# Feed-forward blocks of an encoder trunk: one plain chunk in place of two, and two seven-product chunks opened by p1 and p2

## The chip, the cores and the metric

The kernel runs on one core of a Trainium2 chip. TensorE multiplies matrices, VectorE and ScalarE work element by element, GpSimd (POOL in the profile) and SyncE (SP) mostly issue DMAs here. The metric is the device time of one execution in microseconds (us), the median of several runs. All arithmetic that matters is in float32.

## The reference, cut to what matters

Two batches of tokens, 512 and 256 long, run through two layers with shared weights. Each layer is a feed-forward block, a token mixer, and a second feed-forward block:

```python
def swiglu_ffn(x, w1, w2):
    gate, up = jnp.split(x @ w1, 2, axis=-1)
    return (jax.nn.silu(gate) * up) @ w2
...
x = x + 0.5 * swiglu_ffn(rmsnorm(x, norm_g[li, 0]), ffn_w1[li, 0], ffn_w2[li, 0])
...
x = x + 0.5 * swiglu_ffn(rmsnorm(x, norm_g[li, 2]), ffn_w1[li, 1], ffn_w2[li, 1])
```

The model width is 1024 and the hidden width 2816. So there are four feed-forward blocks, called f0, f1, f2 and f3 here and in the code; the mixers stand between f0 and f1 and between f2 and f3.

## The kernel before, in words

All 768 tokens are worked on at once, split into two halves of 384. A float32 product is made of three fast ones: each operand is split into a high part, rounded to the fast type by a ScalarE copy, and a low part, which VectorE gets by subtracting the high part from the original. TensorE then accumulates high x high, high x low and low x high (`mm3`, and the inner loop of `product`, L522). Line numbers are those of the profile.

**Chunks.** The first multiplication of a feed-forward block goes by 22 chunks of 128 hidden columns. A chunk has a gate part and an up part. There are two kinds:

- A *plain* chunk (`up_plain`, L499) multiplies gate and up for one token half at a time: 2 products over 8 slices of the width, 3 matmuls each, for each of two halves. Its weights are two pieces of 128x1024, each split at once (`plain_steps`, L176).
- A *seven-product* chunk (`up_pair`, L536) takes gate and up by the two halves of the width, and these by the two token halves, as a 2x2 block product, and does it in seven products, p1 to p7, in place of eight, Strassen-Winograd fashion. Each product runs over 4 slices of the width. Each needs one token operand (`FACTOR`, L47): the plain blocks b00, b10, b11, or the mixed ones t1 to t4; and one weight operand, one of the four blocks a11, a12, a21, a22 or a sum of them.

**Weights of a seven-product chunk** (`quad_steps`, L199). Two loads (`wr` tiles, four buffers) bring gate and up. A third load brings a21 a second time (`s3`, two buffers), and two accumulating DMAs on GpSimd's queue (L153) add a11 into `s3` for p7 and a22 into a21. Two VectorE additions (L243) make the operands of p6 (a11 += a21) and p3 (a12 += a11) in place. Each of the seven operands is split: ScalarE cast at L229, VectorE subtraction at L230, into one `w` tile. There are eight `w` tiles. `ahead` stages the next operand whenever a `w` tile is counted free, so the program's order of staging follows the `done` calls of the products.

**Token operands.** At the start of a block the normalized tokens are transposed on TensorE, scaled, and split (`turn`, L398 on; the splits are `put`, whose copy and subtraction are L293 and L294). One call does one half of the width for one half of the tokens. Then `sums` (L450) makes the mixed operands: `mix` (L439) does four subtractions per half of the inner slices (L441, L442, L444, L445) and splits t1, t4, t3 and t2 in this order (L294), all on tiles of 128x768. In f0 two more additions of 128x768 (L453) stand ahead of it. `turn` and `sums` are queued in `self.deferred`, and `run_later` takes one at a time, at set places between the matmuls.

**The order at the start of a block** (`ffn`, L673 on). Chunks 0 and 1 (`PLAIN = 2`) are plain: chunk 0 half 0, chunk 1 half 0, chunk 0 half 1, chunk 1 half 1. While the first 96 matmuls run, the second token half is turned and `sums` is handed in; the b01 and b11 operands are first needed by the second 96. Then come chunks 2 and 3 as seven-product chunks in the order `UP` (p1, p7, p2, p5, p4, p6, p3). The four chunks' results are mixed in the same way (`gather`) for the second multiplication (`down_quad`, L581 on, matmuls at L608), which itself is in seven products per group of four chunks. The remaining 18 chunks are seven-product chunks in four more groups of four and a last pair.

**Who decides the order on an engine.** The program is written in one sequence, and the order of the instructions on each engine is fixed when it is built: of those that can go, the one written first goes first, and one written later gets in where the earlier ones would have to wait. `tc.issue_after(i)` holds an instruction behind `i` on `i`'s engine.

Of the kernel before, what the change touches and what calls it, by code (L numbers as in the profile page):

```python
# [12 lines left out]
AF = mybir.ActivationFunctionType  # L13
# [3 lines left out]
P = 128  # L17
D = 1024
DFF = 2816
NC = D // P  # L20
NF = DFF // P
# [14 lines left out]
H = T // 2  # L36
HB = H // P
PLAIN = 2
GROUPS = (NF - PLAIN) // 4
WBUFS = 8  # L40
# [3 lines left out]
WARM = 21  # L44
UP = ("p1", "p7", "p2", "p5", "p4", "p6", "p3")
DOWN = ("p1", "p2", "p5", "p4", "p7", "p6", "p3")
FACTOR = {"p1": "b00", "p2": "b10", "p3": "b11", "p4": "t4", "p5": "t1", "p6": "t2", "p7": "t3"}  # L47


class Trunk:  # L50
# [104 lines left out]
    def load_next(self):  # L155
# [43 lines left out]
    def quad_steps(self, key, raws, srcs, order):  # L199
# [35 lines left out]
        own = {"p1": [a11], "p2": [a12], "p3": [a12], "p4": [a22], "p5": [a21], "p6": [a11], "p7": s3}  # L235
        sums = {"p6": (a11, a21), "p3": (a12, a11)}
        last = [None]

        def step(name):
            if name in sums:  # L240
                into, term = sums[name]
# [156 lines left out]
    def turn(self, half, part, row):  # L398
# [61 lines left out]
    normed = mixed = first = halved = None  # L460
    normal = None
    plains = 0
# [73 lines left out]
    def up_pair(self, tag, j, hold=False):  # L536
        nc = self.nc
        key = (tag, j)
        a, b, c, d = (self.ps(H) for _ in range(4))
# [8 lines left out]
        self.tail = None  # L548
        p("p7", c, True, False)
        nc.scalar.copy(w, c)  # L550
        free("p7")
        p("p2", a, False, True)
        nc.scalar.activation(a, a, AF.Silu)
        free("p2")
        p("p5", d, True, False)
        nc.vector.tensor_sub(w, w, d)
        free("p5")
        p("p4", c, False, True)
# [4 lines left out]
        free("p4", "p6")  # L563
        yield t
# [13 lines left out]
        free("p3")  # L578
        yield w

    def down_quad(self, tag, g, hid):  # L581
# [91 lines left out]
    def ffn(self, tag, next_row):  # L673
        for g in range(GROUPS):
# [7 lines left out]
            def gather(ts, kp):  # L682
                self.mix(ts[0], ts[1], ts[2], ts[3], lambda name, src: put(name, src, kp))

            if g == 0:
                ts = {}
                for half in range(2):
                    for j in range(PLAIN):
                        t = ts[2 * j + half] = self.up_plain(tag, j, half)
                        name = f"b{j}{half}"  # L690
                        if name != "b01":
                            low = put(name, t, 0)
                        if name == "b00" and self.whole:
                            with self.tc.issue_after(low):
                                for parts in self.whole[:2]:
                                    self.nc.vector.tensor_add(*parts)
                            del self.whole[:2]
                gather(ts, 0)
                self.run_later(len(self.deferred))
            for kp in range(2):  # L700
                if g == 0 and kp == 0:
                    continue
                ts = []
                for j in range(2):
                    for half, t in enumerate(self.up_pair(tag, 4 * g + 2 * kp + j, j == 0)):
                        ts.append(t)
                        name = f"b{j}{half}"
                        if name != "b01":
                            put(name, t, kp)
                gather(ts, kp)  # L710
# [868 lines left out]
```

## Time and profile before

| | |
|---|---|
| median of 3 runs | 2731.82 us (2731.79 to 2732.84) |
| span of the profiled execution | 2730.5 us |
| TensorE busy | 2720.2 us, 17305 matmuls |
| VectorE busy | 2110.3 us |
| ScalarE busy | 1339.0 us |
| GpSimd busy | 204.8 us |

The span is the time from the first to the last instruction in one profiled execution; the runs are timed from outside. In the profile's rows an instruction stands with its line, engine, operation, the tiles that it writes and reads, its shape and a count; behind the bar are busy time and the mean duration of one. In a timeline, a row begins with its start in us from the span's start and the time that it covers; a bracket at the end tells how long the engine had been idle before it and what ended that. ACT is ScalarE, DVE VectorE, PE TensorE's matmuls and PEld its weight loads. Tiles: `big` are token operands, `wr` and `s` raw weights, `w` split weights, `ps` PSUM banks, `tA` intermediate results.

### The profile page before, as it was taken

The page shows a single profiled execution, that of the slowest core. Times are in us where ns is not written, and L with a number is a line of the kernel's source. Part 1 is how long each engine was busy: PE and PEld are TensorE (multiplying, and loading weights), DVE is VectorE, ACT ScalarE, POOL GpSimd, SP SyncE. Part 2 cuts the span into 40 slices and gives each one's busy share as a digit, 9 for nine tenths or more (in the row PEclk, how much of TensorE's full clock was granted, in tenths as well). Part 3 has the DMA queues.
Part 4 walks back from the last instruction along what each step waited for, and adds up shares of the span by engine and source line. Part 5 has one row for each costly group of instructions (what it writes and reads, how often), then busy time and mean ns, then how long its engine had stood idle before and what let it go on. Part 6 is the DMA issues. An engine that isn't in the chain of part 4 may idle for free.

```text
span 2730.5 us, 44549 instructions
## 1 busy us (share of the span) xinstructions
PE 2720.2 (100%) x17305; PEld 2483.8 (91%) x17305; DVE 2110.3 (77%) x3789; ACT 1339.0 (49%) x2507; POOL 204.8 (7%) x243
## 2 busy tenths in 40 slices
PE   9999999999999999999999999999999999999998
PEld 9999999889888889999999999999987789999998
DVE  8888788567476778778888878887847768787877
ACT  6444444456466554444446444444546754444443
POOL 1110110000000000111110011101000000111000
PEclk9999999999999999999999999999999999999999
DMA  6544554311110524465553355544422123555443
GB/s 183 136 123 117 127 143 120 123 56 48 55 41 25 143 65 120 113 147 129 128 121 102 88 129 139 135 116 112 133 72 78 47 62 87 130 139 135 117 112 108
DMA packets 331411, 293.98 MB, mean 108 GB/s; under 512 B 11752, under 2 KB 258240, under 8 KB 331200
## 3 DMA queue, kind: packets, MB, share of 16 engines
q1 hardware_dynamic: 294352, 212.89, 26.6%
q0 software_dynamic: 32544, 64.76, 13.6%
q10 hardware_dynamic: 4304, 13.49, 1.4%
q8 instruction: 135, 2.21, 0.3%
q14 instruction: 76, 0.62, 0.1%
HBM read 216.91 MB, written 9.44 MB: 83 GB/s over the span
## 4 chain that ended last, share of the span: by engine, by line
PE 97%; DVE 1%; ACT 1%; issue 0%; DMA 0%; DVEq 0%; SPq 0%; ACTq 0%
PE ps L527 42%; PE ps L608 21%; PE ps L288 9%; PE ps L289 9%; PE ps L290 9%; PE ps L856 1%; PE ps L643 1%; PE ps L1451 1%; PE ps L1442 1%; PE ps L1004 1%; PE ps L1390 1%; PE ps L411 1%; PE ps L980 0%; PE ps L969 0%; DVE x L671 0%
## 5 line engine op out<-in xcount | busy, mean ns | idle before, releaser
L527 PE MATMUL ps<-big,w 128*128 128x384 f32 x6720 | 1169.7, 334 | 0.6 <-ACT tA L544 0.6
L527 PEld LDWEIGHTS ps<-big,w 128*128 128x128 f32 x6720 | 1165.9, 188 | 2.8 <-ACT tA L544 1.2
L229 ACT CAST w<-wr 128x512 fp32r<-128x512 f32 (+1 forms) x606 | 424.2, 710 | 721.8 <-DVE wr L243 305.4
L230 DVE TENSOR_TENSOR w<-wr,w 128x512 fp32r<-128x512 f32 (+1 forms) x606 | 480.5, 798 | 225.4 <-ACT w L229 158.5
L608 PE MATMUL ps<-w,big 128*128 128x512 f32 x2520 | 575.4, 389 | 0.0
L608 PEld LDWEIGHTS ps<-w,big 128*128 128x128 f32 x2520 | 472.8, 188 | 97.5 <-DVE x L671 0.3
L671 DVE SCALAR_TENSOR_TENSOR x<-ps,x 128x512 f32<-128x512 f32 x468 | 302.6, 681 | 4.7 <-PE ps L290 4.7
L288 PE MATMUL ps<-w,big 128*128 128x512 f32 x576 | 232.5, 404 | 0.0
L290 PE MATMUL ps<-w,big 128*128 128x512 f32 x576 | 225.5, 391 | 0.0
L289 PE MATMUL ps<-w,big 128*128 128x512 f32 x576 | 225.1, 391 | 0.0
L288 PE MATMUL ps<-big,w 128*128 128x384 f32 (+2 forms) x640 | 217.9, 342 | 0.2
L289 PE MATMUL ps<-big,w 128*128 128x384 f32 (+2 forms) x640 | 215.8, 337 | 0.4 <-DVE big L371 0.2
L290 PE MATMUL ps<-big,w 128*128 128x384 f32 (+2 forms) x640 | 215.1, 336 | 0.0
L293 ACT CAST big<-tA 128x384 fp32r<-128x384 f32 x296 | 147.8, 512 | 117.5 <-DVE tA L572 40.4
L153 POOL DMA_DIRECT2D s<-wr x122 | 106.3, 913 | 1300.1 <-DMA wr<-in_ffn_w_dram 623.6
L189 DVE TENSOR_TENSOR w<-wr,w 128x1024 fp32r<-128x1024 f32 (+1 forms) x88 | 105.9, 1209 | 82.0 <-ACT w L186 73.4
L294 DVE TENSOR_TENSOR big<-tA,big 128x384 fp32r<-128x384 f32 x296 | 159.9, 551 | 8.2 <-ACT big L293 7.8
L153 POOL DMA_DIRECT2D wr<-wr x101 | 87.6, 868 | 1009.3 <-DVE tA L1110 386.0
L186 ACT CAST w<-wr 128x1024 fp32r<-128x1024 f32 (+1 forms) x90 | 93.0, 1035 | 93.4 <-PE ps L289 66.3
L288 PEld LDWEIGHTS ps<-w,big 128*128 128x128 f32 x576 | 108.3, 188 | 25.6 <-issue 4.6
L290 PEld LDWEIGHTS ps<-w,big 128*128 128x128 f32 x576 | 108.1, 188 | 23.5 <-issue 0.4
L289 PEld LDWEIGHTS ps<-big,w 128*128 128x128 f32 x640 | 121.0, 189 | 9.4 <-DVE big L294 1.0
(191 smaller groups left out, 2891.8 us busy)
## 6 DMA issues: line engine op xcount, KB each, us to landing
wr<-in_ffn_w_dram SPq DMA_DIRECT2D x264, 512.0 KB, 3.9
s<-wr POOLq DMA_DIRECT2D x122, 256.0 KB, 5.1
s<-in_ffn_w_dram SPq DMA_DIRECT2D x120, 256.0 KB, 3.3
wr<-wr POOLq DMA_DIRECT2D x80, 256.0 KB, 4.2
wr<-in_hg_w_in_dram SPq DMA_DIRECT2D x40, 512.0 KB, 3.8
wr<-wr POOLq DMA_DIRECT2D x21, 512.0 KB, 6.0
spill<-x ACTq DMA_DIRECT2D x12, 512.0 KB, 2.9
x<-spill ACTq DMA_DIRECT2D x12, 512.0 KB, 3.3
```

The source lines that it names most:

```text
L153: self.nc.gpsimd.dma_start(out, src, accum_op=ALU.add)
L189: eng.tensor_sub(lo, raw[:, ks, :], hi.bitcast(F32))
L229: nc.scalar.copy(h, src)
L230: low = nc.vector.tensor_sub(l, src, h.bitcast(F32)).ins
L288: nc.tensor.matmul(out, a[0], b[0], start=first, stop=False)
L289: nc.tensor.matmul(out, a[0], b[1], start=False, stop=False)
L290: nc.tensor.matmul(out, a[1], b[0], start=False, stop=last)
L293: self.nc.scalar.copy(hi, src)
L294: return self.nc.vector.tensor_sub(lo, src, hi.bitcast(F32)).ins
L527: self.nc.tensor.matmul(ps, a[x], b[y], start=first and k == 0 and i == 0, stop=k == 3 and i == 2, skip_group_check=True,)
L608: nc.tensor.matmul(ps, a[x], w[y], start=name == chain and kp == 0 and q == 0, stop=kp == 1 and q == 2, skip_group_check=True,)
L671: return self.nc.vector.scalar_tensor_tensor(x, ps, c, x, ALU.mult, ALU.add).ins
```

## The change

Chunk 1 becomes a seven-product chunk too. Chunks 1 and 2 are opened together by the new function `open_pair`: p1 and p2 of both need only b00 and b10, so they take the place of the plain chunk 1's half 0. Behind plain chunk 0's half 1 come the rest, crossed: p3 of chunk 1, p3 of chunk 2, p5, p7 of chunk 1, p5 of chunk 2, p4, p6 of chunk 1, p7 of chunk 2, then p6 and p4 of chunk 2. Since p3 now runs before p6, both weight additions are made ahead of p3, held behind the last subtraction of `turn` (`self.turned`). The staging of these operands is barred (`self.closed`) until the first product of chunk 0's half 1 is done. Chunk 3 takes its products in the order `THIRD`, with p4 second and p7 fourth. The places at which `run_later` is called move with the products that stand there: of the six calls in the first 96 matmuls, four are now behind p1 and p2 of the two chunks. The bank and the intermediate tiles of the pair are used in another order, with p3 opening the bank that p5 closes.

```diff
-PLAIN = 2
-GROUPS = (NF - PLAIN) // 4
+GROUPS = (NF - 2) // 4
...
+OPEN = ("p1", "p2", "p3", "p5", "p7", "p4", "p6")
+OPEN2 = ("p1", "p2", "p3", "p5", "p7", "p6", "p4")
+THIRD = ("p1", "p4", "p2", "p7", "p5", "p6", "p3")
...
-        self.loaded.append((len(raws), steps))
+        if how is OPEN:
+            self.loaded.append((2, steps[:2]))
+            self.opened = steps[2:]
+        elif how is OPEN2:
+            a, b = self.opened, steps[2:]
+            self.loaded.append((0, steps[:2]))
+            self.closed = (2, [a[0], b[0], a[1], a[2], b[1], a[3], a[4]])
+            self.loaded += [self.closed, (2, b[2:])]
+        else:
+            self.loaded.append((len(raws), steps))
...
-        sums = {"p6": (a11, a21), "p3": (a12, a11)}
+        sums = {"p6": [(a11, a21)], "p3": [(a12, a11)]}
+        if order in (OPEN, OPEN2):
+            sums = {"p3": sums["p6"] + sums["p3"]}
...
-                with self.tc.issue_after(last[0]):
+                low = self.turned if order in (OPEN, OPEN2) else last[0]
+                with self.tc.issue_after(last[0]), self.tc.issue_after(low):
                     nc.vector.tensor_add(into, into, term)
...
+            if self.loaded[0] is self.closed:
+                return
...
             low = self.put(name, kp, self.tn[(part, half)][:, kp])
+            self.turned = low
...
-            if i < PLAIN:
+            if i == 0:
...
-                self.plan_quad((tag, i), (gate, up), (NC, P), UP)
+                self.plan_quad((tag, i), (gate, up), (NC, P), {1: OPEN, 2: OPEN2, 3: THIRD}.get(i, UP))
...
-                if half == 0 and k in (((), (2, 6)), ((3, 7), (3, 7)))[j][c]:
+                if half == 0 and c and k in (2, 6):
                     self.run_later()
             if half:
+                self.closed = None
                 self.done((tag, j, c))
...
+    def open_pair(self, tag, j, hold):
...
+        def gate():
+            p("p1", "a", True, False)
+            nc.scalar.copy(v, banks["a"])
+            free("p1")
+            self.run_later()
+            p("p2", "a", False, True)
+            nc.scalar.activation(banks["a"], banks["a"], AF.Silu)
+            free("p2")
+            self.run_later()
+
+        def p3():
+            p("p3", "d", True, False)
+            nc.scalar.copy(w, banks["d"])
+            free("p3")
+
+        def p5():
+            p("p5", "d", False, True)
+            free("p5")
...
             if g == 0:
...
+                gate, p3, p5, p7, p4, p6, results = zip(*(self.open_pair(tag, j, j == 2) for j in (1, 2)))
+                gate[0]()
+                gate[1]()
+                first.append(self.up_plain(tag, 0, 1))
                 self.run_later(len(self.deferred))
+                for step in (p3[0], p3[1], p5[0], p7[0], p5[1], p4[0], p6[0], p7[1]):
+                    step()
+
+                def second():
+                    p6[1]()
+                    p4[1]()
+                    yield from results[1]()
```

Left out of the diff above are `open_pair`'s p7, p4, p6 and its results, which combine the banks by the same sums and differences as `up_pair` does, and the two places of `up_pair` where chunk 3's p4 and p7 are exchanged.

More of the change, by code (lines that the diff above doesn't have):

```diff
@@ L537, in up_pair @@
         nc = self.nc
+        third = j == 3
         key = (tag, j)
@@ L548, in up_pair @@
         self.tail = None
-        p("p7", c, True, False)
+        p("p4" if third else "p7", c, True, False)
         nc.scalar.copy(w, c)
-        free("p7")
+        free("p4" if third else "p7")
         p("p2", a, False, True)
@@ L554, in up_pair @@
         free("p2")
+        if third:
+            p("p7", c, False, True)
+            nc.vector.tensor_sub(w, c, w)
+            free("p7")
         p("p5", d, True, False)
@@ L557, in up_pair @@
         free("p5")
-        p("p4", c, False, True)
+        if not third:
+            p("p4", c, False, True)
         p("p6", b, True, True)
@@ L562, in up_pair @@
         nc.vector.tensor_mul(t, t, a)
-        free("p4", "p6")
+        free(*(("p6",) if third else ("p4", "p6")))
         yield t
@@ L579, in up_pair, with p, free, p7 @@
         yield w
+    def open_pair(self, tag, j, hold):
+        nc = self.nc
+        banks = {}
+        v, w = (self.tmp(H) for _ in range(2))
+        def p(name, bank, first, last):
+            if first:
+                banks[bank] = self.ps(H)
+            self.product((tag, j), name, FACTOR[name], banks[bank], first, last)
+        def free(name):
+            self.done((tag, j, name))
+        def gate():
[14 more added lines that the diff above has]
+            free("p5")
+        def p7():
+            p("p7", "c", True, False)
+            nc.vector.tensor_add(w, w, banks["c"])
+            nc.vector.tensor_sub(w, w, banks["d"])
+            free("p7")
+        def p4():
+            p("p4", "c", False, True)
+            free("p4")
+        def p6():
+            p("p6", "b", True, True)
+            nc.vector.tensor_sub(v, v, banks["b"])
+            free("p6")
+        def results():
+            t = self.tmp(H)
+            nc.vector.tensor_sub(t, banks["c"], v)
+            nc.vector.tensor_mul(t, t, banks["a"])
+            yield t
+            nc.vector.tensor_sub(w, w, v)
+            nc.vector.tensor_add(v, v, banks["d"])
+            def finish(after=None):
+                with self.tc.issue_after(after) if after else nullcontext():
+                    self.last_act = nc.scalar.activation(v, v, AF.Silu).ins
+                self.last_dve = nc.vector.tensor_mul(w, v, w).ins
+            if hold:
+                self.tail = finish
+            else:
+                finish()
+            yield w
+        return gate, p3, p5, p7, p4, p6, results
     def down_quad(self, tag, g, hid):
@@ L683, in gather @@
                 self.mix(ts[0], ts[1], ts[2], ts[3], lambda name, src: put(name, src, kp))
+            pairs = {}
             if g == 0:
[L686 to L697, printed above, removed]
@@ L698, in ffn @@
-                gather(ts, 0)
-                self.run_later(len(self.deferred))
+                first = [self.up_plain(tag, 0, 0)]
+                low = put("b00", first[0], 0)
+                if self.whole:
+                    with self.tc.issue_after(low):
+                        for parts in self.whole[:2]:
+                            self.nc.vector.tensor_add(*parts)
+                    del self.whole[:2]
+                gate, p3, p5, p7, p4, p6, results = zip(*(self.open_pair(tag, j, j == 2) for j in (1, 2)))
```

14 lines of the change are left out of this document (7 added, 7 removed).

## The prediction

> **What bounds the kernel now.** I read the page first, then the shapes kept apart, then the timelines around the starts of the four feed-forward blocks.
>
> ```profile
> span 2730.5 us, 44549 instructions
> PE 2720.2 (100%) x17305; PEld 2483.8 (91%) x17305; DVE 2110.3 (77%) x3789; ACT 1339.0 (49%) x2507; POOL 204.8 (7%) x243
> L527 PE MATMUL ps<-big,w 128*128 128x384 f32 x6720 | 1169.7, 334 | 0.6 <-ACT tA L544 0.6
> PE ps L104 <- DVE eps L101: 1.1, 1, 1.1
> ```
>
> TensorE is busy for all but 10 us of the span, before the commonest matmul it idled 0.6 us in 6720, and its longest wait, the first row of the waits, is 1.1 us at the very start. So an instruction taken from TensorE is worth its whole pace, until TensorE has to wait. The mean of 334 ns is no pace, since neighbours overlap: 1169.7 us / 6720 = 0.174 us from one to the next. The plain chunks' matmuls have the same shape.
>
> ```profile
> 48.35 29.28 PE L527 MATMUL ps<-big,w 128*128 128x384 f32 x168
> 77.47 28.90 PE L608 MATMUL ps<-w,big 128*128 128x512 f32 x126
> 1030.91 29.28 PE L527 MATMUL ps<-big,w 128*128 128x384 f32 x168
> 1520.87 19.40 PE L527 MATMUL ps<-big,w 128*128 128x384 f32 x111
> 2272.07 18.19 PE L527 MATMUL ps<-big,w 128*128 128x384 f32 x104
> ```
>
> These rows of TensorE's timeline show where, in blocks f0 to f3, the plain chunks end and chunk 2 begins. The first gives the pace again: (77.47 - 48.35) / 168 = 0.173 us. The question is what VectorE does just before, since it makes everything that TensorE reads here.
>
> **The saving.** A plain chunk takes 2 halves x 2 products x 8 x 3 = 96 matmuls, a seven-product chunk 7 x 4 x 3 = 84. Chunk 1 changes kind in four blocks: 4 x 12 x 0.1735 us = 8.3 us. This is certain, and it is the ceiling.
>
> **What moves earlier.** In the old order TensorE runs 192 plain matmuls and then p1 of chunk 2 before it needs a mixed operand (t3, for p7). In the new one it runs 96 matmuls (plain half 0, then p1 and p2 of chunks 1 and 2), 48 of plain half 1, and then p3 of chunk 1, p3 of chunk 2, p5 with t1, p7 with t3. So the plain part ends 48 x 0.1735 = 8.3 us earlier than the five rows say: at 40.0, 1022.6, 1512.5 and 2263.7 us. There p3 of chunk 1 starts. Its third matmul reads the low weight half, so that must exist at 40.4. P3 of chunk 2 starts 12 x 0.1735 = 2.1 us later and needs its low half at 42.4, 1025.0, 1515.0 and 2266.2.
>
> **What p3 costs VectorE.** Two additions (L243), a ScalarE cast, then a subtraction (L230). The change lets the additions start only behind the last operand written by `turn`, and both chunks' p3 are staged in the program behind `sums`, because `closed` opens only after the first plain product of half 1. So, who goes first on VectorE when both are ready?
>
> ```profile
> 35.94 0.62 ACT L229 CAST w<-wr 128x512 fp32r<-128x512 f32 x1 [4.63 <-issue]
> 30.42 1.82 DVE L294 TENSOR_TENSOR big<-big,big 128x768 fp32r<-128x768 f32 x2
> 32.16 1.82 DVE L453 TENSOR_TENSOR big<-big 128x768 f32<-128x768 f32 x2
> 33.90 1.81 DVE L441 TENSOR_TENSOR big<-big,big 128x768 f32<-128x768 f32 x2
> 35.64 1.82 DVE L442 TENSOR_TENSOR big<-big,big 128x768 f32<-128x768 f32 x2
> 37.38 0.95 DVE L444 TENSOR_TENSOR big<-big,big 128x768 f32<-128x768 f32 x1
> 38.24 0.95 DVE L294 TENSOR_TENSOR big<-big,big 128x768 fp32r<-128x768 f32 x1
> 39.11 0.94 DVE L445 TENSOR_TENSOR big<-big,big 128x768 f32<-128x768 f32 x1
> 39.98 0.94 DVE L444 TENSOR_TENSOR big<-big,big 128x768 f32<-128x768 f32 x1
> 40.85 0.54 DVE L519 TENSOR_TENSOR tA<-tA,ps 128x384 f32<-128x384 f32 x1
> 41.97 3.57 DVE L294 TENSOR_TENSOR big<-big,big 128x768 fp32r<-128x768 f32 x4 [0.57 <-ACT big L293]
> 45.45 0.95 DVE L445 TENSOR_TENSOR big<-big,big 128x768 f32<-128x768 f32 x1
> 46.32 0.68 DVE L230 TENSOR_TENSOR w<-wr,w 128x512 fp32r<-128x512 f32 x1
> 46.92 0.68 DVE L230 TENSOR_TENSOR w<-s,w 128x512 fp32r<-128x512 f32 x1
> 47.52 2.69 DVE L294 TENSOR_TENSOR big<-big,big 128x768 fp32r<-128x768 f32 x3
> 50.13 0.55 DVE L294 TENSOR_TENSOR big<-tA,big 128x384 fp32r<-128x384 f32 x1
> ```
>
> This is block f0. The pair at 30.42 ends `turn`; from 32.16 to 50.13 VectorE works off `sums`. The first weight of chunk 2, which the old program stages at the place where the new one stages p3, was cast at 35.94, and its subtraction came at 46.32, about 9.8 us after the cast ended. It got in where the next step of `sums` had to wait for a cast. So staged weights stand behind `sums` and get only its gaps. From start to start a step of 128x768 takes 0.87 us (3.48 / 4 from 41.97) and a weight step 0.60 us (46.32 to 46.92).
>
> **Block f0.** From 32.16, `sums` is 18 steps (L453, L441, L442, L444, L445 twice each, eight L294): 15.7 us. The six p3 steps of two chunks add 3.6: 51.5 us, against a need at 42.4, a wait of 9.1 us. The gaps are those of the rows: one at 40.85, two at 46.32. They take two additions of chunk 1 and one of chunk 2; both subtractions come behind the last three L294, or the first gets in just ahead of one. At most the three final L294 (2.6 us) could fall behind p3 of chunk 2, so 6.5 is the lower end; with a gap lost to a cast it is 10. I take 9.1.
>
> **Blocks f1 to f3.**
>
> ```profile
> 1008.83 0.95 DVE L441 TENSOR_TENSOR big<-big,big 128x768 f32<-128x768 f32 x1
> 1009.70 0.55 DVE L519 TENSOR_TENSOR tA<-tA,ps 128x384 f32<-128x384 f32 x1
> ...
> 1018.26 0.95 DVE L442 TENSOR_TENSOR big<-big,big 128x768 f32<-128x768 f32 x1
> 1019.12 0.68 DVE L230 TENSOR_TENSOR w<-wr,w 128x512 fp32r<-128x512 f32 x1
> ...
> 1023.40 2.69 DVE L294 TENSOR_TENSOR big<-big,big 128x768 fp32r<-128x768 f32 x3
> 1026.01 0.55 DVE L294 TENSOR_TENSOR big<-tA,big 128x384 fp32r<-128x384 f32 x1
> 1498.78 0.95 DVE L441 TENSOR_TENSOR big<-big,big 128x768 f32<-128x768 f32 x1
> 2249.99 0.95 DVE L441 TENSOR_TENSOR big<-big,big 128x768 f32<-128x768 f32 x1
> ```
>
> Here `sums` starts at 1008.83, 1498.78 and 2249.99. There is no L453, so 16 steps make 13.9 us; chunk 0's half 0 adds two steps of 0.46 (1009.70 is one), and p3 adds 3.6, together 18.5 us. The second p3 is ready at 1027.3, 1517.3 and 2268.5, against needs at 1025.0, 1515.0 and 2266.2: 2.3 us late in each. At 1019.12 a weight did slip in ahead of L444, so the first p3 can just make it. If the second passes the final three L294 the wait is nil; with 0.9 us lost to its cast (0.62 long in f0's row) and the way to ScalarE and back, it is 3.2. I take 2.5, nearer the upper end because the rows give weights gaps alone: three times 2.5 is 7.5.
>
> **The rest.** Behind the late p3 the weights come off VectorE at 0.6 us each while TensorE uses one per 2.1 us, and by then t1 to t4 are done: nothing. The new chunk gives VectorE 9 weight steps of 0.60 and 8 evictions and combinations of 0.46 for the old 2 wide subtractions and 2 multiplications, about 6 us more per block.
>
> ```profile
> L189 DVE TENSOR_TENSOR w<-wr,w 128x1024 fp32r<-128x1024 f32 x86 | 104.6, 1221 | 82.0 <-ACT w L186 73.4 <-PE ps L527 7.5
> 11.00:48.35 37.35, 37.08 (x219) 36.09 (x220) 35.12 (x50) 28.25 (x51) 8.96 (x10) 1.00 0.74 183
> 48.35:77.47 29.12, 29.12 (x169) 29.12 (x169) 25.92 (x45) 15.68 (x28) 2.62 (x3) 1.00 0.50 127
> 1031.00:1088.00 57.00, 57.00 (x293) 52.17 (x292) 47.82 (x78) 24.14 (x41) 6.10 (x7) 1.00 0.49 123
> s<-wr POOLq DMA_DIRECT2D x122, 256.0 KB, 5.1
> ```
>
> Behind the length of a stretch stand TensorE, its weight loads and, third, VectorE: in f1 VectorE has 9.2 us free behind the start, which covers the 6. In f0 it has 2.2 + 3.2 = 5.4 us free in 66, so the 6 us fit only because the wait above lengthens the stage; without that cover up to 2.7 us (6.0 + 2.1 - 5.4) would be owed in f0. ScalarE is free for a quarter of that time. Each chunk 1 now issues one more load of 256 KB on SyncE's queue and two accumulating DMAs on GpSimd's, 5.1 us to landing; the additions wait for `turn` anyway, so this is nothing, 1 to 2 us if f0's landings slip. Chunk 3's loads must wait until p6 of chunk 1 is split, five weights or some 4 us behind p3 of chunk 2; but from that p3 to chunk 3's p1 there are nine products, 18.7 us, so 14 us of cover over a landing of some 5. Its p7, which hangs on an accumulating DMA, is moved to fourth place. Nothing, by these covers.
>
> **Sum.** -8.3 + 9.1 + 7.5 = +8.3 us. The profiled span of 2730.5 stands 1.3 below the median of 2731.8, as the same execution outside its instructions; I carry that over: 2740.1 us.
>
> The old trace has no wait over 1.1 us, and the granted clock, the last figure but two of each window, stays at 1.00. The Trainium skill (TensorE: Matmul & The Clock Gate, HAM oscillation) says that a wait over about 3.4 us lets the clock fall to half until TensorE has again been busy for that long. That would add an estimated 1.7 us behind f0's wait, by the page alone: 2741.8; no run here shows it.
>
> **Rivals.** *Full saving:* p3 does not stand behind `sums`. Before p5 must come p3's 3.6 us and the eight steps that lead to t1 in f0 (two each of L453, L441, L442, L294: 7.0 us): 32.16 + 10.6 = 42.8, ahead of p5's 44.2 (40.0 and two products). VectorE has the capacity; only its order is against it. If p3's additions go first or early, TensorE hardly waits, and the time is 2731.8 - 8.3 = 2723.5, faster. It decides when p3 of chunk 2 is ready by 42.4 and 1025. For it: the rows show an order made for the old program, where no weight was urgent. Against it: the 35.94 to 46.32 row pair. *Half:* f1 to f3 fit p3 into their four gaps, f0 waits 6.5 to 9.1: 2731.8 - 8.3 + 7.8 = 2731.3, no change. *Worse:* as forecast, and f0's waits run to 10, the others to 3.2, with a further 2 us because chunk 3 or the down products inherit VectorE's arrears: 2731.8 - 8.3 + 10 + 9.6 + 2 = 2745. *Clock:* as forecast, and TensorE comes back from f0's wait at a lower clock; p3's twelve matmuls at half pace cost 12 x 0.1735 = 2.1 us: 2742.2. The rows speak neither way, since nothing waited that long.
>
> **How the numbers follow.** Forecast 0.41, its own range 2736 to 2743 (waits of 6.5 and 3 x 2.0, or of 10 and 3 x 3.2). Full saving 0.30, half 0.13, worse 0.10, clock 0.06. A measurement of this kernel can tell about 0.2%, 5.5 us, from no change. The forecast's lower edge falls inside that, so 0.03 of it counts as no change: faster 0.30, same 0.16, slower 0.54. The range must reach from the full saving to the worse case: 2723 to 2745.
>
> **What would show it.** Right, if the new trace has TensorE idle before the first p3 of f0 for some 7 us, released by a weight's subtraction (L230's successor) that ran behind the last L294 of `sums`, and again by 2 to 3 us in f1 to f3; if the seven-product matmuls number 7056; if VectorE is solid from 16 to 55 us. Wrong, if p3's additions stand ahead of L442 or L444, or if TensorE's idle time in the four starts sums to under 3 us. If it waits instead before chunk 3 or the down products, the arrears were the cost and p3 was not.

## The result and the profile after

The changed kernel takes 2756.61 us (median of 4 runs, 2755.37 to 2757.02) against 2731.81 for the kernel before: ratio 1.0089, 95% interval 1.0075 to 1.0103. It is slower by 24.8 us. The forecast was 2740.1 with a range of 2723 to 2745: the direction was right, the size was not. One execution of run e2 below took 3864 us at a granted clock of 0.654, where its others have 0.998 or 0.999, and is left out of that run's figures.

Line numbers have moved. The seven-product matmul is now L544 (L527 before), the down matmul L699 (L608); a weight's cast and subtraction are L240 and L241 (L229, L230), the weight additions L256 (L243), the token operands' cast and subtraction L308 and L309 (L293, L294); `mix` is L457 to L461 (L441 to L445). L638 and L639 are new: they read chunk 1's and chunk 2's p7 and p5 banks on VectorE. The first lines of the page:

```profile
span 2755.1 us, 44569 instructions
...
PE 2724.0 (99%) x17257; PEld 2480.1 (90%) x17257; DVE 2136.4 (78%) x3849; ACT 1351.1 (49%) x2535; POOL 211.7 (8%) x251
...
PE 88%; DVE 7%; DMA 2%; ACT 2%; issue 1%; SPq 0%; DVEq 0%; ACTq 0%; POOLq 0%
...
L544 PE MATMUL ps<-big,w 128*128 128x384 f32 x7056 | 1241.2, 336 | 21.1 <-ACT w L240 15.7
```

There are 48 matmuls fewer, as the change means to have it (17305 - 17257), and 336 more of them are seven-product matmuls. But their row now has 21.1 us of idle time before it, where it had 0.6, and the chain of work that ended last, which was TensorE for 97%, runs through VectorE and the DMAs for 9%. The share of busy time hardly says so: 99% for 100%.

All of the loss lies at the four block starts. From the first plain matmul of a block to the last matmul of its first down group (start to start; called the block's first part below) it took:

| us | f0 | f1 | f2 | f3 |
|---|---|---|---|---|
| before | 94.9 | 94.1 | 94.2 | 94.1 |
| after | 105.8 | 98.5 | 98.6 | 99.2 |

The differences sum to 24.8 us, though each block also has 2.1 us of matmuls less. TensorE's timeline has the waits; the bracket gives the idle time before the row and what ended it:

```profile
39.78 0.34 PE L305 MATMUL ps<-big,w 128*128 128x384 f32 x1
48.72 1.01 PE L544 MATMUL ps<-big,w 128*128 128x384 f32 x2 [8.60 <-ACT w L240]
50.28 12.02 PE L544 MATMUL ps<-big,w 128*128 128x384 f32 x52 [0.56 <-DVE w L241]
...
1037.84 7.39 PE L544 MATMUL ps<-big,w 128*128 128x384 f32 x31 [2.43 <-ACT w L240]
...
1532.36 17.09 PE L544 MATMUL ps<-big,w 128*128 128x384 f32 x96 [2.23 <-ACT w L240]
1551.50 4.75 PE L544 MATMUL ps<-big,w 128*128 128x384 f32 x26 [2.06 <-DVE tA L638]
...
2288.55 18.49 PE L544 MATMUL ps<-big,w 128*128 128x384 f32 x96 [2.43 <-ACT w L240]
2308.04 4.25 PE L544 MATMUL ps<-big,w 128*128 128x384 f32 x23 [1.00 <-DVE tA L638]
```

The waits for L240 and L241 stand before p3: 16.2 us in all. Those for L638 stand before chunk 2's p4, which adds to the bank that L638 must first have read. VectorE's timeline in f0 shows the first kind:

```profile
40.79 0.68 DVE L256 TENSOR_TENSOR wr<-wr,wr 128x512 f32<-128x512 f32 x1
41.40 3.55 DVE L309 TENSOR_TENSOR big<-big,big 128x768 fp32r<-128x768 f32 x4
44.87 0.95 DVE L461 TENSOR_TENSOR big<-big,big 128x768 f32<-128x768 f32 x1
45.74 0.68 DVE L256 TENSOR_TENSOR wr<-wr 128x512 f32<-128x512 f32 x1
46.34 0.68 DVE L256 TENSOR_TENSOR wr<-wr,wr 128x512 f32<-128x512 f32 x1
46.95 2.68 DVE L309 TENSOR_TENSOR big<-big,big 128x768 fp32r<-128x768 f32 x3
49.55 0.68 DVE L241 TENSOR_TENSOR w<-wr,w 128x512 fp32r<-128x512 f32 x1
50.15 0.68 DVE L256 TENSOR_TENSOR wr<-wr 128x512 f32<-128x512 f32 x1
51.52 1.29 DVE L241 TENSOR_TENSOR w<-wr,w 128x512 fp32r<-128x512 f32 x2 [0.22 <-ACT w L240]
```

TensorE stands still from 40.1 us while VectorE, never idle, works off `sums`; p3's additions get the gaps that the prediction named, and the first subtraction comes behind the last three L309. The first two matmuls of p3 read only the high half of the weight; the 8.60 us end with its cast, the 0.56 us behind them with its subtraction.

The second kind was not foreseen. These are SyncE, GpSimd, ScalarE and then VectorE in f2, in the timeline:

```profile
1535.47 3.49 SPq L166 DMA_DIRECT2D wr<-in_ffn_w_dram  x4
...
1541.01 0.88 POOL L155 DMA_DIRECT2D s<-wr  x1 [53.06 <-DMA wr<-in_ffn_w_dram]
...
1547.20 0.62 ACT L240 CAST w<-s 128x512 fp32r<-128x512 f32 x1 [3.83 <-DMA s<-wr]
...
1547.85 0.69 DVE L241 TENSOR_TENSOR w<-s,w 128x512 fp32r<-128x512 f32 x1 [3.68 <-ACT w L240]
1548.46 0.55 DVE L648 TENSOR_TENSOR tA<-tA,ps 128x384 f32<-128x384 f32 x1
1549.13 0.69 DVE L241 TENSOR_TENSOR w<-wr,w 128x512 fp32r<-128x512 f32 x1
1549.74 0.68 DVE L256 TENSOR_TENSOR wr<-wr,wr 128x512 f32<-128x512 f32 x1
1550.35 0.55 DVE L653 TENSOR_TENSOR tA<-ps,tA 128x384 f32<-128x384 f32 x1
1550.81 0.54 DVE L638 TENSOR_TENSOR tA<-tA,ps 128x384 f32<-128x384 f32 x1
```

Chunk 3's loads are issued from 1535.47 on, its accumulating DMA at 1541.01, and the sum lands when ScalarE can cast it, at 1547.20. VectorE's next instruction is that weight's subtraction, so VectorE idles 3.68 us; the reading of the bank (L638) is five places behind it. TensorE does not need this weight yet: chunk 2's p4 and chunk 3's p1, p4 and p2 come first, 4 x 2.1 = 8 us. It needs L638, and L638 is stuck behind the weight.

A third thing shows in the windows behind the waits (behind the length of a window stand the busy times of TensorE, its weight loads, VectorE, ScalarE and GpSimd; the last figure but two is the granted clock):

```profile
49.00:56.40 7.40, 6.84 (x21) 6.34 (x22) 7.18 (x12) 4.63 (x9) 0.00 (x0) 0.51 0.16 46
1037.84:1044.00 6.16, 6.16 (x25) 5.94 (x26) 5.58 (x9) 4.59 (x9) 0.00 (x0) 0.72 0.38 106
1532.36:1538.00 5.64, 5.64 (x31) 5.42 (x32) 5.49 (x9) 4.49 (x9) 0.00 (x0) 1.00 0.35 93
...
2288.55:2294.00 5.45, 5.45 (x22) 5.42 (x23) 5.00 (x9) 4.59 (x9) 0.00 (x0) 0.69 0.25 68
```

TensorE comes back at a lower clock, with matmuls 0.32 us apart for 0.174, in f0, f1 and f3 but not in f2. By the windows, busy time times the missing share of the clock, that costs an estimated 6.84 x 0.49 + 6.16 x 0.28 + 5.45 x 0.31 = 6.8 us.

So the span's 24.6 us come together as: -8.3 for the matmuls, 21.1 of waits (16.2 before p3, 3.2 before p4, 1.3 behind a ScalarE copy, 0.4 of small ones), 6.8 of lower clock, and some 3.0 for eleven restarts: the last matmul before a wait takes its whole 0.34 us, as the row at 39.78 shows, in place of 0.17, and the one behind it starts 0.1 late. That makes 22.6; 2.0 us are not assigned one by one. Most of them are slower matmuls too: the 1008 seven-product matmuls of the four stretches take 186.0 us without the waits, 11.3 more than at 0.1733 us each, where clock and restarts explain 9.8.

### The profile page after: what moved, and what is told of

Read it like the earlier page. It is cut to its first block, busy times and chain, and to the rows that moved or that the text cites. A ratio compares the mean times of both kernels' runs of the same rounds, so it can differ in the third digit from the quotient of the medians.

```text
span 2755.1 us, 44569 instructions
## 1 busy us (share of the span) xinstructions
PE 2724.0 (99%) x17257; PEld 2480.1 (90%) x17257; DVE 2136.4 (78%) x3849; ACT 1351.1 (49%) x2535; POOL 211.7 (8%) x251
## 4 chain that ended last, share of the span: by engine, by line
PE 88%; DVE 7%; DMA 2%; ACT 2%; issue 1%; SPq 0%; DVEq 0%; ACTq 0%; POOLq 0%
PE ps L544 39%; PE ps L699 19%; PE ps L303 7%; PE ps L304 7%; PE ps L305 7%; DVE big L309 1%; PE ps L955 1%; DVE w L241 1%; PE ps L734 1%; PE ps L1550 1%; PE ps L1541 1%; PE ps L1103 1%; PE ps L1489 1%; DMA wr<-wr 1%; DMA wr<-in_ffn_w_dram 1%
## 5 line engine op out<-in xcount | busy, mean ns | idle before, releaser
L544 PE MATMUL ps<-big,w 128*128 128x384 f32 x7056 | 1241.2, 336 | 21.1 <-ACT w L240 15.7
L544 PEld LDWEIGHTS ps<-big,w 128*128 128x128 f32 x7056 | 1229.6, 189 | 29.8 <-ACT w L240 21.5
L240 ACT CAST w<-wr 128x512 fp32r<-128x512 f32 (+1 forms) x630 | 437.5, 707 | 700.2 <-DVE wr L256 309.4
L241 DVE TENSOR_TENSOR w<-wr,w 128x512 fp32r<-128x512 f32 (+1 forms) x630 | 496.2, 795 | 212.6 <-ACT w L240 147.2
L699 PE MATMUL ps<-w,big 128*128 128x512 f32 x2520 | 576.2, 389 | 0.0
L699 PEld LDWEIGHTS ps<-w,big 128*128 128x128 f32 x2520 | 472.4, 188 | 97.7
L308 ACT CAST big<-tA 128x384 fp32r<-128x384 f32 x296 | 148.0, 513 | 131.8 <-DVE tA L585 38.2
L303 PE MATMUL ps<-big,w 128*128 128x256 f32 (+2 forms) x512 | 174.7, 343 | 0.1
L304 PE MATMUL ps<-big,w 128*128 128x256 f32 (+2 forms) x512 | 173.0, 338 | 0.5 <-DVE big L386 0.2
L305 PE MATMUL ps<-big,w 128*128 128x256 f32 (+2 forms) x512 | 172.1, 336 | 0.0
L309 DVE TENSOR_TENSOR big<-tA,big 128x384 fp32r<-128x384 f32 x296 | 160.3, 553 | 7.5 <-ACT big L308 6.6
L200 DVE TENSOR_TENSOR w<-wr,w 128x1024 fp32r<-128x1024 f32 (+1 forms) x80 | 96.2, 1208 | 80.7 <-ACT w L197 74.9
L303 PEld LDWEIGHTS ps<-w,big 128*128 128x128 f32 x576 | 108.3, 188 | 25.7 <-issue 4.6
L305 PEld LDWEIGHTS ps<-w,big 128*128 128x128 f32 x576 | 108.1, 188 | 23.6 <-issue 0.4
L197 ACT CAST w<-wr 128x1024 fp32r<-128x1024 f32 (+1 forms) x82 | 84.5, 1033 | 90.5 <-PE ps L304 66.5
L304 PEld LDWEIGHTS ps<-w,big 128*128 128x128 f32 x576 | 108.4, 188 | 19.6
```

What stands on the lines that cost most here:

```text
L200: eng.tensor_sub(lo, raw[:, ks, :], hi.bitcast(F32))
L240: nc.scalar.copy(h, src)
L241: low = nc.vector.tensor_sub(l, src, h.bitcast(F32)).ins
L303: nc.tensor.matmul(out, a[0], b[0], start=first, stop=False)
L304: nc.tensor.matmul(out, a[0], b[1], start=False, stop=False)
L305: nc.tensor.matmul(out, a[1], b[0], start=False, stop=last)
```

## The experiments

Theory 1: p3 behind `sums` on VectorE is the cost, with the clock behind its waits. Rival: something else stands right behind it and takes its place.

**e1: p3 first.** At the head of `sums`:

```diff
+        if self.closed:
+            for _ in range(2):
+                self.stage_next()
```

> The changed kernel with one edit: both chunks' p3 are staged in the program just ahead of the sums of the token operands, not behind them. Theory (p3's weights stand behind the sums on VectorE): the waits before p3, 9.2 us in f0 and 2.2 to 2.4 in f1 to f3, go almost wholly, and with them the stretches at half clock (some 9 us); the later waits before p4 of chunk 2 stay. About 2756.6 - 16.3 - 9 = 2731, within 4. Rival (VectorE has not the capacity, so that the wait only moves from p3 to the mixed operands of p5 and p7): TensorE waits as long a product or two later, 2745 to 2757.

Measured: 2754.53 us (ratio 1.0080, 1.0065 to 1.0095). The table of waits (total, times, longest):

```profile
PE ps L547 <- DVE tA L641: 16.7, 4, 5.4
PE ps L547 <- DVE w L241: 2.3, 3, 1.3
```

The waits for p3's weights are gone but for 2.3 us in f0, so their cause was named rightly. But the waits before p4 (L641 here) have grown from 3.2 to 16.7 us. The time lies where the rival put it; the waits do not stand, but for 0.4 us in f0, before p5 and p7, where want of capacity on VectorE would have put them. In f0 VectorE idles 4.61 us at a weight subtraction that reads `s`, with L641 right behind it. Two bounds lay one behind the other.

**e2: TensorE kept busy.** Behind `up_plain`'s second half, matmuls into a bank that nobody reads, 44 in f0 and 10 in the others:

```diff
+                spare, fill = self.ps(H), self.operand("b00", 0)
+                for _ in range(44 if tag == "f0" else 10):
+                    self.nc.tensor.matmul(spare, self.identr, fill[0], start=True, stop=True)
```

> The changed kernel with matmuls added that nothing reads: 44 in f0 and 10 in f1 to f3, behind plain chunk 0's half 1 and ahead of p3, where TensorE waits. They take 7.6 us of f0's wait of 9.2 and 1.7 of the others' 2.4. Theory (the matmuls after a wait run at half the clock because of the wait): the half-clock stretches of some 4, 2.5 and 2.5 us go, 2756.6 - 9 = 2748. Rival (the slow pace behind the waits comes from late weights, one by one): the same pace, no change, 2755 to 2758. A cost of 1 to 2 us is possible where the added matmuls outlast a wait.

Measured: 2761.05 us (1.0106, 1.0089 to 1.0122), a miss for both. The windows behind p3's waits in f0 and f1:

```profile
49.00:57.00 8.00, 7.06 (x30) 6.74 (x31) 7.45 (x13) 5.42 (x11) 0.00 (x0) 0.79 0.17 45
1039.00:1046.00 7.00, 6.05 (x34) 5.83 (x35) 6.18 (x11) 5.43 (x11) 0.00 (x0) 1.00 0.32 86
```

With the wait of f1 cut to 1.09 us the clock stays at 1.00, and so it does behind p3's waits of 1.09 us in f2 and f3: the half rate does come from the wait. But the time was not won: the 74 added matmuls take 13.0 us where the waits before p3 fell by 11.1, and the waits before p4 rose from 3.2 to 7.7 us. What TensorE gained it lost again at L638.

**e3: chunk 3's later weights staged later.** They may be staged only once chunk 2's p7 products are read:

```diff
+        elif how is THIRD:
+            self.barred = (2, steps[3:])
+            self.loaded += [(0, steps[:3]), self.barred]
...
+            if self.loaded[0] is self.closed or self.loaded[0] is self.barred:
                 return
```

> The changed kernel with chunk 3's weights from p7 on barred from staging until VectorE has read the bank of chunk 2's p7. Theory (before p4 of chunk 2 TensorE waits for that read, which stands on VectorE behind chunk 3's p7 weight, whose cast waits for an accumulating DMA): the waits of 0.2, 2.1 and 1.0 us in f1 to f3 go, 2756.6 - 4 = 2753. Rival (VectorE is simply behind with evictions): no change, or slower by some us because chunk 3's own weights come late.

Measured: 2756.61 us (1.0089, 1.0074 to 1.0104), no change. The waits before p4 sum to 2.5 us for 3.2 and have changed places (2.28 us in f1). The edit did not do what it was meant to do: in f1 VectorE still idles 4.09 us at the weight's subtraction, with the reading of the bank five places behind it. So this settles nothing. Being written later does not keep the weight behind a reading that is not ready when the order is made.

**e4: e1 and e3 together.**

> Both edits, p3 ahead of the sums and chunk 3's p7 barred. If the two waits are separate, the gains add up: 2731 - 4 = 2727, within 4, so faster than the kernel before the change by 1 to 8 us. If VectorE's capacity is the limit, 2740 or more.

Measured: 2751.58 us (1.0074, 1.0057 to 1.0090). VectorE's timeline in f1 (L244 is the weight's subtraction, L644 the reading of the bank):

```profile
1049.37 0.69 DVE L244 TENSOR_TENSOR w<-s,w 128x512 fp32r<-128x512 f32 x1 [4.30 <-ACT w L243]
...
1052.23 0.55 DVE L644 TENSOR_TENSOR tA<-tA,ps 128x384 f32<-128x384 f32 x1
```

Again the weight from the accumulating DMA is ahead, with 4.30 us of idle time. The time is one that the expectation gave to want of capacity, but an engine that idles has capacity. From here on theory 2: what costs is the place of chunk 3's weights in VectorE's order, not VectorE's work, and it must be fixed there.

**e5: the p7 weight's subtraction fixed behind the reads.**

```diff
+                held = self.read if order is THIRD and name == "p7" else None
+                with self.tc.issue_after(held) if held else nullcontext():
                     low = nc.vector.tensor_sub(l, src, h.bitcast(F32)).ins
```

`self.read` is the second read of chunk 2's banks (`w - d` in p7).

> As e4_both (the p3 steps of chunks 1 and 2 ahead of sums; chunk 3's p7 weight staged only after the pair's p7 products are read), but now the subtraction that makes the low part of chunk 3's p7 weight is also fixed in VectorE's own order behind the two reads of chunk 2's banks, so that it can't stand at the head of VectorE's order while its DMA is under way. Theory (VectorE's order is blocked by a weight whose DMA is late): the wait before chunk 2's p4 (2.60, 4.18, 3.10 and 3.18 us in e4_both) goes in all four blocks, the half-rate matmuls behind the waits go with it, some 2.7 us of short waits stay in the first block, and the time is about 2727 us, 2724 to 2733. Rival (the transfer itself sets the time, wherever its reader stands): the wait shows up again ahead of chunk 3's p7 products or on another queue, and the time is 2745 to 2752.

Measured: 2751.80 us (1.0073, 1.0057 to 1.0088), a miss. ScalarE and VectorE in f2 (L646 is the read):

```profile
1545.41 0.62 ACT L243 CAST w<-wr 128x512 fp32r<-128x512 f32 x1 [2.14 <-DMA wr<-wr]
...
1546.07 0.69 DVE L246 TENSOR_TENSOR w<-wr,w 128x512 fp32r<-128x512 f32 x1 [4.58 <-ACT w L243]
...
1547.74 0.54 DVE L646 TENSOR_TENSOR tA<-tA,ps 128x384 f32<-128x384 f32 x1
```

The source is now `wr`, not `s`: the p5 weight, which rests on the other accumulating DMA, has taken the place at the head.

**e6: the same hold without e1.**

> The changed kernel with the hold alone: chunk 3's p7 weight is staged after, and its subtraction ordered behind, the two reads of chunk 2's banks; the p3 steps stay behind sums. Theory (two separate costs): the waits before p3 stay as they are, 16.2 us in all, with the half-rate matmuls behind them, and the waits before chunk 2's p4 (0.16, 2.06 and 1.00 us) go: about 2752 us, 2749 to 2755. Rival (one cost that merely moves): 2756 or above.

Measured: 2755.73 us (1.0086, 1.0071 to 1.0101), just short of the rival's figure. The waits before p3 stay at 16.2 us and those before p4 at 3.2, otherwise divided (1.36 us in f1, 1.83 in f2). A miss for the theory as it was put; but as in e5 the hold left the p5 weight free (in f2 VectorE idles 3.04 us for it, with the reading behind it), so it decides nothing between them.

**e8: e1 with chunk 3 in its old order**, so that "p7 later" is undone.

```diff
-        third = j == 3
+        third = False
...
-{1: OPEN, 2: OPEN2, 3: THIRD}.get(i, UP)
+{1: OPEN, 2: OPEN2}.get(i, UP)
```

> As e1_p3_first (the p3 steps ahead of sums), but chunk 3 keeps the order of products and weights that it has in the kernel before, p7 second: this undoes the one part 'the next chunk's p7 later'. Theory (the late weight blocks VectorE ahead of chunk 2's p4): the p7 weight is now wanted two products sooner and stands still earlier in VectorE's order, so the waits before chunk 2's p4 stay at 3 to 6 us a block or grow: 2754 to 2765 us. Rival (the reordering of chunk 3 is itself what put the late weight in the way): the waits before p4 go, 2725 to 2735 us.

Measured: 2755.66 us (1.0084, 1.0068 to 1.0101). The waits before p4 are 4.63, 4.50 and 3.50 us in f1 to f3. So chunk 3's new order is not what put the late weight in the way; it is late in either order.

**e9: both late weights held**, p7's and p5's, casts and subtractions.

```diff
-                held = self.read if order is THIRD and name == "p7" else None
+                held = self.read if order is THIRD and name in ("p7", "p5") else None
                 with self.tc.issue_after(held) if held else nullcontext():
+                    nc.scalar.copy(h, src)
```

> As e5_both_held, but both weights of chunk 3 that rest on an accumulating DMA, p7's and p5's, have their cast and their subtraction ordered behind the two reads of chunk 2's banks (in e5_both_held the p5 weight took the place of the p7 weight: VectorE idled 4.58 us for it with the read of the bank queued behind it). Theory (head-of-line wait of VectorE on chunk 3's weights): the waits before chunk 2's p4 in the second, third and fourth blocks (3.97, 3.38 and 2.69 us) go, and some 7 us of half-rate matmuls with them; the first block's order is not changed by this edit and keeps its 3.32 us: about 2735 us, 2732 to 2740. Rival (chunk 3's transfers themselves are too late for its products): the wait moves on to chunk 3's p7 or p5, and the time stays at 2745 to 2753 us.

Measured: 2742.75 us (1.0037, 1.0023 to 1.0052), 9 us less than e5. The waits before p4 in f1 to f3 are gone, no half rate is left there, and the three first parts fall from 98.2, 99.0 and 96.2 to 94.3, 94.9 and 95.8 us. ScalarE and VectorE in f2:

```profile
1540.12 0.62 ACT L245 CAST w<-s 128x512 fp32r<-128x512 f32 x1 [4.22 <-DMA s<-wr]
...
1539.96 0.55 DVE L646 TENSOR_TENSOR tA<-tA,ps 128x384 f32<-128x384 f32 x1
...
1541.36 0.68 DVE L246 TENSOR_TENSOR w<-s,w 128x512 fp32r<-128x512 f32 x1
```

ScalarE still waits 4.22 us for the sum in `s` (3.69 in e5). Counted from the block's first matmul, the casts of the two late weights start at 46.0 and 47.8 us, in e5 at 45.5 and 48.2: the transfers are as late as they were. But the read is now ahead of the weights and runs at once. This is the run that decides for theory 2. The expectation was 2735: single waits of 0.4 to 2.0 us came up at other places, and f0 stands at 105.8 (105.1 in e5).

**e10: p6 and p3 of chunk 3 later as well**, behind ScalarE's copy of chunk 3's p4 products.

```diff
-            self.barred = (2, steps[3:])
-            self.loaded += [(0, steps[:3]), self.barred]
+            self.barred = [(0, steps[3:5]), (2, steps[5:])]
+            self.loaded += [(0, steps[:3]), *self.barred]
...
+        copied = nc.scalar.copy(w, c).ins
+        if third:
+            self.barred = ()
+            self.copied = copied
```

> As e9_held_two, but the last two weights of chunk 3, p6 and p3, are also staged later: behind ScalarE's copy of chunk 3's p4 products, which in the first block stood behind the cast of the p6 weight (3.32 us before the p7 products). Theory: the first block's wait goes too, and the time is about 2730 us, 2726 to 2735. Rival (the raw buffers are now freed later still, so the loads of the first down group come late): a wait of 2 us or more appears ahead of chunk 3's p6 or of the first down group in each block, and the time is 2740 us or more.

Measured: 2741.34 us (1.0032, 1.0020 to 1.0044). The first parts of the blocks: 104.3, 94.7, 94.5, 93.7. Its waits and two windows:

```profile
PE ps L555 <- ACT tA L573: 2.8, 2, 2.4
PE ps L555 <- DVE w L246: 2.2, 3, 1.3
PE ps L716 <- DVE x L779: 2.0, 4, 0.7
```

```profile
40.00:58.00 18.00, 15.26 (x81) 13.50 (x80) 18.00 (x26) 9.17 (x14) 0.00 (x0) 1.00 0.15 44
...
1535.00:1550.00 15.00, 15.00 (x87) 14.72 (x86) 12.85 (x27) 5.97 (x13) 2.32 (x4) 1.00 0.71 181
```

The expectation was 2730. In f1 to f3 the loss is gone, and yet little is won. Their stretches hold three matmuls of the next chunk more than before, which now stand ahead of the last down matmul; without these 0.5 us they take 94.2, 94.0 and 93.2 us. The rest of the 2.1 us of matmuls saved in a block goes into waits of up to 0.7 us, most before the down products, into restarts and into small differences of pace. In f0 9.4 us are left (0.5 of them such matmuls), and the wait that this edit was aimed at, before chunk 3's p7, fell only from 3.32 to 2.36 us. There VectorE, third in the window after TensorE and its weight loads, is busy for all of the 18 us from 40 to 58; in the other blocks it has time over.

**e11: the first block as before, the others as in e10.** Where `tag == "f0"`, `ffn` and `up_plain` run the code of the kernel before.

```diff
-            if i == 0:
+            if i < (2 if tag == "f0" else 1):
...
-        third = j == 3
+        third = j == 3 and tag != "f0"
```

> As e10_held_three in the second, third and fourth feed-forward blocks; the first block has the order of the kernel before (two plain chunks, no opened chunks). Theory (what is left of the loss in e10_held_three lies in the first block alone, where VectorE was busy in 18.0 of the 18 us from 40 to 58 us and TensorE waits for it): the first part of the first block goes back from 104.3 to 94.9 us, the other three stay at about 94.3, and the time is 2732 us, 2729 to 2734, no different from the kernel before. Rival (the other blocks lose too, in parts that the block lengths do not show): 2736 us or more. A gain of more than 2 us on the kernel before is expected by neither: the 2.1 us of matmuls saved in a block are eaten by 1 to 2 us of short waits there.

Measured, in 11 runs: 2731.50 us against 2732.71, ratio 0.9996, 0.9987 to 1.0005. This is the best form found, and it cannot be told from the kernel before. The first parts are 95.2, 95.1, 94.8 and 94.2: f0's loss went with its order, the others tie. (They sum to 2.0 us more than before, but 1.6 of these are the nine matmuls of next chunks that f1 to f3 hold here too; the profiled span, 2730.1, is 0.4 less.)

**e12: e10 with f0 eased**: the additions of `sums` over `self.whole` on GpSimd, and the hold of p7 and p5 in f0 moved behind chunk 1's results.

```diff
-                self.nc.vector.tensor_add(*parts)
+                self.nc.gpsimd.tensor_add(*parts)
```

> As e10_held_three, with two things changed in the first block alone: two of the additions of 128x768 that VectorE makes there ahead of the mixed operands are given to GpSimd, and chunk 3's p7 and p5 weights are ordered behind the results of chunk 1. Theory (in the first block VectorE has no free time between 40 and 58 us, so each us taken from it there shortens the waits of TensorE): the early waits (1.27, 0.42, 0.31 and 0.63 us) fall by about 1.7 us in sum, the wait of 2.36 us ahead of chunk 3's p7 goes with its half-rate matmuls, the first part of the first block falls from 104.3 to about 98 us and the time to about 2735 us. Rival (GpSimd's addition takes longer than VectorE's and the mixed operands wait for it; or the late transfers of chunk 3 set the block's length wherever their readers stand): the block stays at 103 us or grows, and the time is 2740 us or more.

Measured: 2742.10 us (1.0033, 1.0021 to 1.0046), as the rival had it; f0's first part grew to 107.3. VectorE, GpSimd and ScalarE in f0:

```profile
30.62 5.61 DVE L316 TENSOR_TENSOR big<-big,big 128x768 fp32r<-128x768 f32 x2
...
30.58 3.95 POOL L479 TENSOR_TENSOR big<-big 128x768 f32<-128x768 f32 x2
...
70.03 0.62 ACT L245 CAST w<-wr 128x512 fp32r<-128x512 f32 x1 [3.69 <-DMA wr<-wr]
...
74.25 0.47 ACT L573 COPY tA<-ps 128x384 f32<-128x384 f32 x1
```

Two subtractions that take 1.82 us in the rows of before took 5.61 while GpSimd added, and TensorE waited 1.28 us for the first of them. And the wait ahead of chunk 3's p7 products, for the copy at 74.25, grew from 2.36 to 3.82 us: ScalarE stood 3.69 us at the cast of the held p5 weight, with the results' casts and the copy queued behind. The same wait in line, on the other engine. So what VectorE's full 18 us alone cost in f0 stays open: this run put a new delay in the place of the one that it took away.

## Why the prediction was right in direction and wrong in size

- *The saving, -8.3 us.* Right: 48 matmuls fewer.
- *p3 behind `sums`, +9.1 and 3 x 2.5 = 16.6.* Right in mechanism and size: 9.16 us in f0, 2.43, 2.23 and 2.43 in f1 to f3, 16.25 in all. The additions sit in the gaps that were named, at 40.79, 45.74 and 46.34. In f0 the wait stands before chunk 1's p3 and not chunk 2's, and the fit of 9.1 to 9.16 is in part luck: by the same working chunk 1's subtraction ends some 1.2 us before 51.5, at 50.3 against a need at 40.4, so 9.9 us late. The third matmul of p3, at 50.28, was in fact some 10 us late, 9.16 of it idle time and the rest slow matmuls.
- *"Chunk 3's loads must wait until p6 of chunk 1 is split ... so 14 us of cover over a landing of some 5. Its p7 ... is moved to fourth place. Nothing, by these covers."* This step failed: a term put at nothing. First, a load and an accumulating DMA stand in a row: 1535.47 to 1547.20 is 11.7 us in f2, not 5. Second, the cover was counted to where TensorE uses the weight, and there it held: no wait for that weight's own product is in the trace. But the order on VectorE is fixed, and the reader of the late weight stood ahead of reads that TensorE needed 8 us sooner. It cost 3.2 us in the changed kernel; e1 shows that another 13.5 stood ready behind the first cost, and e9 that it is the place in the order.
- *The length of a wait as its whole price.* In size this is the step that failed most: the sum has a wait at its idle time alone. The clock was a rival with a chance of 0.06, at 2.1 us and in f0 alone; restarts are nowhere. The clock cost about 6.8 us, of which 3.4 in f0, and the restarts about 3.0, together 9.8 of the 16.5 us that the forecast was short. Waits of 2.43 us set the clock off in f1 and f3. The Trainium skill (TensorE: Matmul & The Clock Gate, HAM oscillation) puts the limit at a wait of about 3.4 us, which would have left f1 to f3 at full rate; here the measurement decides.
- *VectorE's arrears in f0, nothing.* Not separated. The prediction saw 2.7 us owed if the wait before p3 should go; in e10 it is gone and f0 is 9.4 us longer than before.
- *The range.* Its upper end took the worse case, 2745, from longer waits of the same kind and 2 us of arrears. It had no term for a second, independent wait, nor for the clock behind short waits. Between the forecast of +8.3 and the result of +24.8 lie 16.5 us: 4.5 of waits behind chunk 3's late weights and the copies, 6.8 of lower clock, 3.0 of restarts, and 2.2 not assigned. The full saving (2723.5) was not within reach by p3's order alone, as e1 shows.

## What to carry to other kernels

When a change makes a transfer later, it isn't enough that it lands before its product: look where its reader stands in the order of VectorE and ScalarE, and what is queued behind that reader. Where TensorE was never idle before, price each new wait at its length and 0.3 us for the restart, and expect from about 2 us on some 1.5 us of half rate or more on top. And when one wait is taken away, ask what would have been late next: here a second bound stood right behind the first, and removing the first won 2 us until the second was gone as well.

## What the runs showed of the hardware

**The clock falls behind waits shorter than expected, and it depends on when they come.** Over the traces of the changed kernel and the experiments, in the four stretches: none of 16 waits of 1.0 to 1.64 us was followed by a stretch of matmuls 0.32 us apart, 13 of 21 waits of 1.83 to 3.18 us were, and all of 16 from 3.26 us up. Such a stretch begins 0 to 2 us after the wait and holds mostly 10 matmuls, 3.2 us, sometimes 16 or 17. A wait of 1.83 us in e6 had one, one of 3.10 us in e4 had none. The records of the granted clock show a pattern: in each trace its changes lie whole multiples of 3.41 us apart. Three such stretches, two around f1's wait of 2.43 us and one at f2's of 2.23 us:

```profile
1035.91:1039.32 3.41, 1.48 (x7) 1.26 (x8) 3.19 (x6) 2.17 (x6) 0.00 (x0) 1.00 0.00 0
1039.32:1042.73 3.41, 3.41 (x13) 3.41 (x12) 3.40 (x6) 3.02 (x7) 0.00 (x0) 0.50 0.37 96
1530.84:1534.25 3.41, 1.89 (x10) 1.67 (x11) 3.19 (x7) 2.56 (x5) 0.00 (x0) 1.00 0.02 5
```

In f1, TensorE idled 1.93 us of one stretch, and the next ran at 0.50. In f2 the wait was cut in two by the grid, no stretch had more than 1.52 us of it, and the clock stayed. Laid on this grid, none of the 21 of these waits that left at most 1.70 us of idle time in any one stretch was followed by the lower clock, all 28 with 1.94 us or more were (a short one in e8 among them, which shares its stretch with the long wait behind it), and of the four between, two. Two waits of 0.96 and 0.94 us in f0 of e2, which fell into one stretch, set it off too. No run moved a wait over the grid on purpose. The Trainium skill (TensorE: Matmul & The Clock Gate, What's actually happening) describes a window of about 3.4 us that runs freely, whatever the kernel does. That the outcome varies with the moment and that a stretch lasts about 3.4 us agrees with that; that some 1.9 us of idle time, little more than half such a window, is enough is not in it.

**GpSimd's additions stop VectorE's subtractions.** In e12, VectorE's two subtractions with both inputs in SBUF took 5.61 us in place of 1.82 while two GpSimd additions ran for 3.95; all of the delay is in the first, which took 4.74 us and ended after both additions, the second 0.94. The Trainium skill (SBUF — State Buffer, SBUF: two separate sides) says that such a VectorE operation and a GpSimd operation that reads SBUF lock each other out for whole instructions; the 3.8 us lost agree with it.
